# Sums of squares without a POOL adder: one change in three places of a two-layer decoder kernel

## The chip, the cores and the metric

The kernel runs on one core of one Trainium2 chip, in one launch. The metric is the device time of an execution in microseconds (us). The engines are named as in the profile: PE (matrix products), PEld (its weight loads), ACT, DVE and POOL (element-wise work), SP (which starts the DMA transfers). The kernel before takes 683.92 us, the median of three runs (682.63 to 685.81).

## What is computed

Two decoder layers over 512 positions of width 1024, in float32. Cut to what the change touches:

```python
def rmsnorm(x, g):
    return x * rsqrt(mean(x * x, axis=-1) + EPS) * g

# layer 1, latent attention
proj = rmsnorm(x, ln_g) @ w_in                  # 1024 -> 384 + 256 + 32 + 1024
c_q, c_kv, k_rope, gate = split(proj)
q  = rmsnorm(c_q,  q_norm_g)  @ w_q_up          # 16 heads of 96
kv = rmsnorm(c_kv, kv_norm_g) @ w_kv_up         # keys and values, 16 heads of 64
x  = x + (softmax_attention(q, k, v) * silu(gate)) @ w_out
x  = x + sigmoid(x @ ple_w_gate[0]) * (p[0] @ ple_w_proj[0])
# shared keys and values of layer 2, stick-breaking attention
k_sh, v_sh = split(rmsnorm(x, kv_ln_g) @ w_kv_shared)
q, gate = split(rmsnorm(x, sb_ln_g) @ sb_w_in)
x = x + (stick_breaking(q, k_sh, v_sh) * silu(gate)) @ w_out2
x = x + sigmoid(x @ ple_w_gate[1]) * (p[1] @ ple_w_proj[1])
```

Four norms need a sum of squares per position: over x, c_q and c_kv in layer 1, and over the new x in between.

## The kernel before

Activations lie transposed: 128 features on the partitions, 512 positions along a row, so x is 8 tiles (`NK`) and the positions are 4 blocks of 128 (`NT`). Each operand is split into a high part (ACT) and a rest (DVE or POOL), and each product is three matmuls (`mm3`, L132): high by high, high by rest, rest by high. The norm is never applied ahead of a product: its sum of squares is taken beside it, and the factor goes in when the product is read out.

A sum over features is a sum over partitions, which the kernel takes with PE: 128 squares per position as the weights, a column of ones as the moving operand (`self.mm(..., rhs=self.ones[:, 0:1])`). A float32 product of that kind is two passes in the trace.

The order on each engine comes from a scheduler that simulates the program, except where `self.lin` ties every PE instruction to the one ahead of it: at the start (L860 to L892), between the layers (L932 on) and in the second attention layer. The three places of the change lie there.

**Place 1, the start.** `mla_in` (L309) runs over k, the 8 tiles of x. Each k loads a tile of x (L330) and a tile of weights (L335), splits both (L163/L164, L343/L344; from k = 2 on POOL makes the rest of the weights) and issues 15 matmuls into 5 accumulators. ACT also squares each tile of x (L322, L325) and POOL adds the squares up (L326), in turn with its splits. Then the 5 accumulators (3 of c_q, 2 of c_kv) are split and squared; POOL adds the squares again, to one tile for c_q and one for c_kv (L368). After `k_rope` (16 matmuls) `stats` (L372) makes 3 x 4 one-column products from the three sum tiles, and only then `mla_group` (L464) begins: 4 tiles of q, 9 matmuls of 384 columns each, then `k_rotate` (first transposes L423), then keys and values. A generator hands these out in steps of 3 matmuls (`next(first)`).

**Place 2, between the layers.** `out_ple` writes the new x; ACT squares each tile (L926, L929), POOL adds 6 of the 8 squares, three tiles stay (`sqs`). PE makes the first key tile of the shared keys (8 steps, tile g), then 12 one-column products (L947), then the second key tile (8 steps, tile s), then `row_of` (L198) transposes the finished factor into a row. The factor is one small power on POOL (L950); the keys are read out only once the row is there (`self.late`).

**Place 3, the end of the second attention layer.** `sb_layer` (L701) runs 26 turns. Each turn hands out filler steps (`fill`) from a generator of other products, in six parts (`marks`), between scores, transposes (`pt_evac`) and the two products with the values (`av`, L573). In the last turn (i = N + 1) no scores and no transposes are left: two `av` of the last pair of heads and seven filler steps. An `av` needs the rest of its weights from DVE (L571, tile `ptl`).

Of the kernel before, what the change touches and what calls it, by code (L numbers as in the profile page):

```python
# [6 lines left out]
F32 = mybir.dt.float32  # L7
# [9 lines left out]
P = 128  # L17
# [61 lines left out]
class Trunk:  # L79
# [229 lines left out]
    def mla_in(self):  # L309
        nc, A = self.nc, self.A  # L310
        gc = self.const([P, NCOL], F32, "gc")
        self.gc = gc
        MC = (QL + KL) // P
        tags = "ggssttt"
        acc = [self.ps([P, S], x) for x in tags[:MC]]
        xacts = []
        sqx = self.t([P, S], F32, "f")
        xss = []

        def square(k):  # L320
            if k == 0:
                nc.scalar.activation(sqx, xss[k], AF.Square)  # L322
            else:
                sq = self.t([P, S], F32, "f")
                nc.scalar.activation(sq, xss[k], AF.Square)  # L325
                nc.gpsimd.tensor_tensor(out=sqx, in0=sqx, in1=sq, op=ALU.add)  # L326

        for k in range(NK):
            xg = self.t([P, S + 8], F32, "e")[:, 0:S + 1]
            nc.sync.dma_start(out=xg, in_=A["xT"][k])  # L330
            xs, gx = xg[:, 0:S], xg[:, S:S + 1]
            cuts = (0, P, QL + KL) if k == 0 else (0, QL + KL)
            ws = self.t([P, QL + KL], F32, "ws")
            for a, b in zip(cuts, cuts[1:]):
                nc.sync.dma_start(out=ws[:, a:b], in_=A["w_c"][k][:, a:b])  # L335
            if k == 2:
                nc.sync.dma_start(out=gc, in_=A["gain_cols"])
            if k == 0:
                xh, xl = self.split_act(xs, "A", scale=gx)
            wh = self.t([P, QL + KL], F32R, "wh")  # L340
            wl = self.t([P, QL + KL], F32R, "wl")
            for a, b in zip(cuts, cuts[1:]):
                nc.scalar.copy(out=wh[:, a:b], in_=ws[:, a:b])  # L343
                (nc.vector if k < 2 else nc.gpsimd).tensor_tensor(out=wl[:, a:b], in0=ws[:, a:b], in1=f32(wh[:, a:b]),  # L344
                                                                  op=ALU.subtract)
            if k > 0:
                xh, xl = self.split_act(xs, "A", scale=gx)
            xacts.append((xh, xl))
            for m in range(MC):
                self.mm3(acc[m], wh[:, m * P:(m + 1) * P], wl[:, m * P:(m + 1) * P], xh, xl, k == 0, k == NK - 1)  # L350
            xss.append(xs)
            if k > 0:
                square(k - 1)
        square(NK - 1)
        self.xacts = xacts
        self.load_small()
        sqs = []
        lats = []
        for m in range(MC):
            lats.append(self.split_act(acc[m], "B", scale=gc[:, C_QN + m:C_QN + m + 1]))  # L360
            if m in (0, QL // P):
                sq = self.t([P, S], F32, "f")
                nc.scalar.activation(sq, acc[m], AF.Square)
                sqs.append(sq)
            else:
                s2 = self.t([P, S], F32, "f")
                nc.scalar.activation(s2, acc[m], AF.Square)
                nc.gpsimd.tensor_tensor(out=sqs[-1], in0=sqs[-1], in1=s2, op=ALU.add)  # L368
        self.cq, self.ckv = lats[:QL // P], lats[QL // P:]
        self.sums = [sqx] + sqs  # L370

    def stats(self):  # L372
        nc = self.nc
        sps = self.ps([P, 3, NT], "t")
        for i, sq in enumerate(self.sums):
            for t in range(NT):
                self.mm(sps[:, i, t:t + 1], lhsT=sq[:, t * P:(t + 1) * P], rhs=self.ones[:, 0:1], start=True,
                        stop=True)
        st = self.const([P, 3, NT], F32, "stats")
        v = nc.vector  # L380
        v.tensor_copy(out=st, in_=sps)
        w = self.const([P, 8, NT], F32, "statw")
        vx, vq, vkv, exx, euq, t0, skv2, krc = [w[:, i] for i in range(8)]
        v.tensor_scalar(out=vx, in0=st[:, 0], scalar1=1.0 / D, scalar2=EPS, op0=ALU.mult, op1=ALU.add)
        v.tensor_scalar(out=exx, in0=vx, scalar1=EPS, scalar2=None, op0=ALU.mult)
        v.scalar_tensor_tensor(out=vq, in0=st[:, 1], scalar=1.0 / QL, in1=exx, op0=ALU.mult, op1=ALU.add)
        v.scalar_tensor_tensor(out=vkv, in0=st[:, 2], scalar=1.0 / KL, in1=exx, op0=ALU.mult, op1=ALU.add)
        v.tensor_scalar(out=euq, in0=vq, scalar1=EPS, scalar2=None, op0=ALU.mult)
        self.euq = euq
        sx = self.const([P, 2, NT], F32, "sxkv")  # L390
        nc.gpsimd.tensor_tensor(out=sx[:, 0], in0=vx, in1=self.mhalf.to_broadcast((P, NT)), op=ALU.pow)
        nc.gpsimd.tensor_tensor(out=sx[:, 1], in0=vkv, in1=self.mhalf.to_broadcast((P, NT)), op=ALU.pow)
        self.sx, self.skv = sx[:, 0], sx[:, 1]
        v.scalar_tensor_tensor(out=skv2, in0=self.skv, scalar=1.0 / QK, in1=self.skv, op0=ALU.mult, op1=ALU.mult)
        self.skv2 = skv2
        self.krw = (t0, krc)
        hs = self.const([QK, 1], F32, "hs")
        nc.vector.memset(hs, QK ** -0.5)
        nc.vector.scalar_tensor_tensor(out=hs[0:HD], in0=self.hg[0:HD, 0:1], scalar=QK ** -0.5,
                                       in1=self.hg[0:HD, 1:2], op0=ALU.mult, op1=ALU.mult)  # L400
        self.hs = hs
# [299 lines left out]
    def sb_layer(self, windows, pair):  # L701


        NU = 3
        GS = NU * GH // 2
        N = NU * NH // 2
        bs, ready = {}, None
        for i in range(N + 2):
            w = min(i // GS, len(windows) - 1)
            n, gen = windows[w]  # L710
            turns = GS if w < len(windows) - 1 else GS + 2
            step = i - w * GS
            quota = n * (step + 1) // turns - n * step // turns
            marks = [quota * x // 6 for x in range(7)]
            if i == N:
                self.cyc = "gs"

            def fill(a, z):
                for _ in range(marks[z] - marks[a]):
                    next(gen, None)  # L720
            if i < N:
                m, u = divmod(i, NU)
                qs, ks, V = self.groups[i // GS]
                bs[i] = self.sb_front(u, self.sb_scores(u, qs[m], ks[m]))
            fill(0, 1)
            if ready is not None:
                self.av(2 * ready, self.groups[ready // 2][2])
            fill(1, 3)
            b = i - 1
            if 0 <= b < N:  # L730
                e = bs.pop(b)
                self.pt_evac(2 * (b // NU), b % NU, e[0])
            fill(3, 4)
            if ready is not None:
                self.av(2 * ready + 1, self.groups[ready // 2][2])
                pair(ready)
                ready = None
            fill(4, 5)
            if 0 <= b < N:
                self.pt_evac(2 * (b // NU) + 1, b % NU, e[1])  # L740
                if b % NU == NU - 1:
                    ready = b // NU
                if i == N:
                    self.split_later()
            fill(5, 6)
            if step == turns - 1:
                for _ in gen:
                    pass
# [103 lines left out]
    def run(self):  # L852
# [23 lines left out]

        grp = lambda g: self.mla_group(g, self.groups[g])
        self.k_rope()
        self.stats()
        self.rope_tables()  # L880
        self.cyc = SPREAD
        first = grp(0)
        for _ in range(3 * NT):
            next(first)
        self.k_rotate()
        for _ in first:
# [56 lines left out]
            next(first)  # L943
        sps = self.ps([P, NT], "t")
        for t in range(NT):
            for i, sq in enumerate(sqs):
                self.mm(sps[:, t:t + 1], lhsT=sq[:, t * P:(t + 1) * P], rhs=self.ones[:, 0:1], start=i == 0,  # L947
                        stop=i == len(sqs) - 1)
        v.tensor_scalar(out=r2, in0=sps, scalar1=1.0 / D, scalar2=EPS, op0=ALU.mult, op1=ALU.add)
        nc.gpsimd.tensor_tensor(out=r2, in0=r2, in1=self.mhalf.to_broadcast((P, NT)), op=ALU.pow)  # L950
        for _ in range(NK):
            next(first)
        self.R2 = self.row_of(r2)
        for f in self.late:
# [40 lines left out]
def pack(inp):  # L995
# [10 lines left out]

    o = {}
    o["xT"] = c(np.concatenate([f["x"][0].T.reshape(NK, P, S), f["mla_ln_g"][0].reshape(NK, P, 1)], axis=2))
    o["pT"] = c(f["p"][:, 0].reshape(2, S, 2, P).transpose(0, 3, 2, 1))
    o["positions"] = c(f["positions"][0].reshape(NT, P).T)  # L1010
    o["gain_cols"] = c(np.concatenate([cols(f["mla_ln_g"][0]), cols(f["mla_q_norm_g"][0]), cols(f["mla_kv_norm_g"][0]),
# [37 lines left out]
```

## Time and profile before

| | |
|---|---|
| median of three runs | 683.92 us |
| the profiled execution, its own time | 683.51 us |
| its span, first to last instruction | 681.7 us |
| PE busy | 666.2 us, 98% of the span |
| DVE, ACT, POOL busy | 476.7, 400.7, 356.8 us |
| mean granted clock of PE | 0.992 |

The span is what the trace shows; 1.8 us of the execution's time lie around it. PE's busy time is close to the span, so a gain must come out of the few gaps of PE, out of instructions that it runs, or out of the stretches in which it ran at the lower of its two clock levels. A granted clock of 1.00 is 2.4 GHz, 0.50 is 1.2 GHz.

### The profile page before, as it was taken

How to read it: one execution, taken by the hardware profiler on the slowest of the kernel's cores; microseconds unless marked ns; L12 is line 12 of the kernel's file. 1: busy time of each engine (PE TensorE's matmuls, PEld its weight loads, DVE VectorE, ACT ScalarE, POOL GpSimd, SP SyncE). 2: the span in 40 equal slices, each digit the busy share in tenths (PEclk: the TensorE clock that was granted, in tenths of full speed). 3: DMA queues.
4: the chain of work that ended last, by engine and by line, in shares of the span. 5: the costliest groups of instructions: out<-in, count | busy, mean ns of one | idle time of the engine just before them, and what ended most of it. 6: DMA issues, size and time to landing. Idle time of an engine off the chain costs nothing.

```text
span 681.7 us, 10052 instructions
## 1 busy us (share of the span) xinstructions
PE 666.2 (98%) x3598; PEld 560.9 (82%) x3598; DVE 476.7 (70%) x868; ACT 400.7 (59%) x812; POOL 356.8 (52%) x293
## 2 busy tenths in 40 slices
PE   8989999999998999999999999999999999999997
PEld 6778898989877888888789788779879877788886
DVE  6866489987986774846853886876886889654332
ACT  7266496987988664444533666566665777432221
POOL 5737678776795550035443663775856677100130
PEclk9989999999999999999989999999999999999999
DMA  7331302100133110734332222111221222442321
GB/s 242 116 120 56 109 32 66 62 17 17 35 110 105 62 62 32 210 118 136 119 128 62 94 87 67 59 68 34 91 67 59 64 93 84 162 125 93 107 80 62
DMA packets 21762, 59.82 MB, mean 88 GB/s; under 512 B 2896, under 2 KB 3664, under 8 KB 21712
## 3 DMA queue, kind: packets, MB, share of 16 engines
q1 hardware_dynamic: 21712, 59.18, 26.9%
q8 instruction: 28, 0.46, 0.3%
q14 instruction: 22, 0.18, 0.1%
HBM read 54.97 MB, written 4.19 MB: 87 GB/s over the span
## 4 chain that ended last, share of the span: by engine, by line
PE 89%; ACT 4%; DVE 4%; issue 1%; POOL 1%; DMA 0%; ACTq 0%; POOLq 0%
PE g L127 41%; PE t L127 25%; PE s L127 16%; PE t L130 6%; DVE A L161 1%; ACT L447 1%; ACT wh L143 1%; DVE e L609 1%; DVE ptl L571 0%; DMA e<-in_xT 0%; POOL f L326 0%; DVE f L804 0%; ACT L611 0%; ACT f L447 0%; ACT e L611 0%
## 5 line engine op out<-in xcount | busy, mean ns | idle before, releaser
L127 PE MATMUL g<-A,wh 128*128 128x512 f32 x560 | 182.6, 405 | 2.1 <-ACT f L802 1.4
L143 ACT CAST wh<-ws 128x1024 fp32r<-128x1024 f32 (+2 forms) x92 | 90.2, 982 | 106.3 <-issue 41.0
L144 DVE TENSOR_TENSOR wl<-ws,wh 128x1024 fp32r<-128x1024 f32 (+2 forms) x72 | 96.8, 1346 | 47.0 <-ACT wh L143 45.9
L127 PEld LDWEIGHTS g<-A,wh 128*128 128x128 f32 x560 | 99.6, 189 | 25.4 <-issue 3.2
L127 PE MATMUL g<-A,wl 128*128 128x512 f32 x280 | 110.9, 396 | 0.7 <-POOL wl L344 0.7
L182 POOL TENSOR_TENSOR ws<-ws,gc 128x1024 f32<-128x1024 f32 x24 | 52.2, 2177 | 62.7 <-DMA ws<-in_w_sq 25.2
L698 POOL TENSOR_TENSOR e<-e,e 128x384 f32<-128x384 f32 (+1 forms) x48 | 61.9, 1309 | 20.0 <-DVE e L697 17.1
L570 ACT CAST pth<-t 128x384 fp32r<-128x384 f32 (+1 forms) x96 | 49.6, 518 | 32.0 <-PE t L130 31.3
L571 DVE TENSOR_TENSOR ptl<-t,pth 128x384 fp32r<-128x384 f32 (+1 forms) x96 | 56.5, 593 | 14.8 <-ACT pth L570 14.3
L127 PEld LDWEIGHTS g<-A,wl 128*128 128x128 f32 x280 | 52.9, 189 | 13.2 <-POOL wl L344 1.6
L127 PE MATMUL t<-A,wh 128*128 128x512 f32 (+1 forms) x192 | 59.1, 393 | 0.0
L130 PE MATMUL t<-ident,e 128*128 128x128 f32 x320 | 55.4, 272 | 0.0
L697 DVE TENSOR_TENSOR_SCAN e<-e,maskb 128x384 f32<-128x384 f32 (+1 forms) x32 | 45.8, 1471 | 8.2 <-ACT e L686 8.2
L130 PEld LDWEIGHTS t<-ident,e 128*128 128x128 f32 x320 | 40.4, 140 | 7.3 <-POOL e L614 0.2
L144 POOL TENSOR_TENSOR wl<-ws,wh 128x1024 fp32r<-128x1024 f32 (+2 forms) x20 | 40.0, 2002 | 12.2 <-ACT wh L143 10.7
L127 PE MATMUL s<-qk,qk 96*128 96x256 f32 (+1 forms) x192 | 44.4, 338 | 1.4 <-ACT qk L548 0.7
L614 POOL TENSOR_SCALAR e<-e,sm 128x384 f32<-128x384 f32 (+3 forms) x48 | 27.6, 579 | 33.3 <-DVE sm L612 28.7
L611 ACT ACTIVATE e<-e,sm 128x128 f32<-128x128 f32 (+1 forms) x64 | 36.3, 568 | 12.6 <-DVE sm L609 10.8
L127 PE MATMUL g<-wh,B 128*128 128x384 f32 (+1 forms) x136 | 43.4, 376 | 0.3 <-DVE v L538 0.3
L127 PE MATMUL g<-wh,A 128*128 128x256 f32 x208 | 42.4, 289 | 0.0
L127 PEld LDWEIGHTS t<-A,wh 128*128 128x128 f32 (+1 forms) x192 | 35.1, 184 | 8.3
L127 PE MATMUL t<-ptl,v 128*128 128x256 f32 (+2 forms) x128 | 39.5, 329 | 1.8 <-DVE ptl L571 1.8
(291 smaller groups left out, 1607.2 us busy)
## 6 DMA issues: line engine op xcount, KB each, us to landing
ws<-in_w_pg SPq DMA_DIRECT2D x16, 512.0 KB, 3.6
ws<-in_w_g SPq DMA_DIRECT2D x8, 512.0 KB, 3.2
ws<-in_w_o SPq DMA_DIRECT2D x16, 256.0 KB, 2.6
ws<-in_w_k SPq DMA_DIRECT2D x8, 512.0 KB, 3.6
ws<-in_w_sq SPq DMA_DIRECT2D x8, 512.0 KB, 3.5
ws<-in_w_v SPq DMA_DIRECT2D x8, 512.0 KB, 3.6
ws<-in_w_sg SPq DMA_DIRECT2D x8, 512.0 KB, 3.5
ws<-in_w_o SPq DMA_DIRECT2D x8, 512.0 KB, 3.6
```

Of the source, the lines that this page charges most:

```text
L127: return self.pe(self.nc.tensor.matmul(*a, **kw))
L130: return self.pe(self.nc.tensor.transpose(*a))
L143: nc.scalar.copy(out=wh, in_=src)
L144: lo_engine.tensor_tensor(out=wl, in0=src, in1=f32(wh), op=ALU.subtract)
L161: (lo_engine or nc.vector).tensor_tensor(out=lo, in0=src, in1=f32(hi), op=ALU.subtract)
L182: nc.gpsimd.tensor_tensor(out=ws, in0=ws, in1=gain.unsqueeze(2).to_broadcast((P, nk, P)), op=ALU.mult)
L570: nc.scalar.copy(out=views[0], in_=ps)
L571: nc.vector.tensor_tensor(out=views[1], in0=ps, in1=f32(views[0]), op=ALU.subtract)
L611: nc.scalar.activation(e[:, 0:n], e[:, 0:n], AF.Exp, bias=st[:, 0:1], scale=-1.0, accum_out=st[:, 2:3])
L614: nc.gpsimd.tensor_scalar(out=e[:, 0:n], in0=e[:, 0:n], scalar1=st[:, 3:4], scalar2=1.0, op0=ALU.mult, op1=ALU.mult)
L697: v.tensor_tensor_scan(out=x, data0=x, data1=mask[:, ::-1], initial=0.0, op0=ALU.mult, op1=ALU.max)
L698: nc.gpsimd.tensor_tensor(out=b[:, 0:n], in0=b[:, 0:n], in1=om[:, 1:n + 1], op=ALU.mult)
```

## The change

Place 1: the squares of x no longer go through PE and POOL. A second copy of x with the positions on the partitions (`x_rows`, 4 blocks of 128 x 1024, 2.1 MB in all) is loaded after the loads of k = 3, and ACT squares each block in place and adds along the row in the same instruction (`accum_out`). POOL's adds L326 and L368 go; the five squares of c_q and c_kv stay five tiles, and `stats` now makes 4 x (3 + 2) one-column products that accumulate in PSUM. `stats` is moved behind the first tile of q, and after each block of positions it takes a step of the following q tile. The small work on the sum of x (its variance, its power) is free to move ahead of `stats`.

Place 2: before each block's three one-column products a step of the second key tile is taken (4 steps), and after them 9 steps instead of 8, so that `row_of` comes 5 steps later than before, inside the first query tile.

Place 3: in the last turn the first `av` comes two filler steps later, the second three.

```diff
-        sqx = self.t([P, S], F32, "f")
-        xss = []
-        def square(k):
-            if k == 0:
-                nc.scalar.activation(sqx, xss[k], AF.Square)
-            else:
-                sq = self.t([P, S], F32, "f")
-                nc.scalar.activation(sq, xss[k], AF.Square)
-                nc.gpsimd.tensor_tensor(out=sqx, in0=sqx, in1=sq, op=ALU.add)
+        st = self.st = self.const([P, 3, NT], F32, "stats")
+        xr = None
+        def square(t):
+            x = xr[t // 2][:, t % 2]
+            nc.scalar.activation(x, x, AF.Square, accum_out=st[:, 0, t:t + 1])
...
+            if k == 3:
+                xr = [self.t([P, 2, D], F32, "v") for _ in range(2)]
+                for t in range(NT):
+                    nc.sync.dma_start(out=xr[t // 2][:, t % 2], in_=A["x_rows"][t])
+            if k >= NK - NT:
+                square(k - NK + NT)
...
-                nc.gpsimd.tensor_tensor(out=sqs[-1], in0=sqs[-1], in1=s2, op=ALU.add)
+            sq = self.t([P, S], F32, "f")
+            nc.scalar.activation(sq, acc[m], AF.Square)
+            self.sums.append(sq)
...
+    def sum_squares(self, ps, t, sqs):
+        for i, sq in enumerate(sqs):
+            self.mm(ps, lhsT=sq[:, t * P:(t + 1) * P], rhs=self.ones[:, 0:1], start=i == 0, stop=i == len(sqs) - 1)
+    def stats(self, steps):
+        sps = self.ps([P, 2, NT], "t")
+        for t in range(NT):
+            self.sum_squares(sps[:, 0, t:t + 1], t, self.sums[:QL // P])
+            self.sum_squares(sps[:, 1, t:t + 1], t, self.sums[QL // P:])
+            next(steps)
...
+            lag = 2 if i == N + 1 else 0
-            fill(0, 1)
+            fill(0, 1 + lag)
...
-            fill(3, 4)
+            fill(3, 4 + lag)
...
-        self.stats()
         first = grp(0)
-        for _ in range(3 * NT):
+        for _ in range(3):
+            next(first)
+        self.stats(first)
+        for _ in range(3 * NT - 3 - NT):
             next(first)
...
         for t in range(NT):
-            for i, sq in enumerate(sqs):
-                self.mm(...)
+            next(first)
+            self.sum_squares(sps[:, t:t + 1], t, sqs)
...
-        for _ in range(NK):
+        for _ in range(NK - NT + 5):
             next(first)
         self.R2 = self.row_of(r2)
```

How the orders differ: outside the three places PE's order is the same instruction for instruction. PE at place 1 before, from the end of `k_rope` (`wh_396`) to the first q tile (g), with the three sum tiles as f:

```order
L127 MATMUL t_399<-A_331,wh_396 64x512 x2
L127 MATMUL t_418<-ones,f_120 128x1 x4
L127 MATMUL t_418<-ones,f_365 128x1 x4
L127 MATMUL t_418<-ones,f_385 128x1 x4
L127 MATMUL g_506<-wh_499,B_361 128x384
```

The same place now, from the last matmuls of the first q tile (g) into the second (s):

```order
L127 MATMUL g_463<-wh_456,B_358 128x384
L127 MATMUL t_478<-ones,f_369 128x1
L127 MATMUL t_478<-ones,f_371 128x1
L127 MATMUL t_478<-ones,f_373 128x1
L127 MATMUL t_478<-ones,f_375 128x1
L127 MATMUL t_478<-ones,f_377 128x1
L127 MATMUL s_484<-wh_456,B_349 128x384
L127 MATMUL s_484<-wl_457,B_349 128x384
L127 MATMUL s_484<-wh_456,B_350 128x384
L127 MATMUL t_478<-ones,f_369 128x1
```

One block of twelve products ahead of all q tiles has become four blocks of five, with three matmuls between them, behind the first q tile.

ACT in `mla_in` before, at k = 2 to 5 (A is a split tile of x, wh a split weight tile, f a square):

```order
L163 ACTIVATE A_186<-e_177 128x512
L325 ACTIVATE f_233<-e_177 128x512
L343 CAST wh_182<-ws_179 128x640
L163 ACTIVATE A_215<-e_207 128x512
L325 ACTIVATE f_262<-e_207 128x512
L163 ACTIVATE A_244<-e_236 128x512
L325 ACTIVATE f_291<-e_236 128x512
L343 CAST wh_211<-ws_209 128x640
```

ACT at the same k now (v is a block of rows of x, stats the sums):

```order
L163 ACTIVATE A_185<-e_176 128x512
L340 CAST wh_181<-ws_178 128x640
L163 ACTIVATE A_211<-e_203 128x512
L340 CAST wh_207<-ws_205 128x640
L323 ACTIVATE v_229,stats<-v_229 128x1024
L323 ACTIVATE v_229,stats<-v_229 128x1024
L323 ACTIVATE v_230,stats<-v_230 128x1024
L323 ACTIVATE v_230,stats<-v_230 128x1024
L163 ACTIVATE A_243<-e_235 128x512
L340 CAST wh_239<-ws_237 128x640
```

The four row squares stand in one piece ahead of everything that k = 4 needs. On SP their four loads stand at the same point, ahead of the loads of k = 4; on DVE two small operations on the sums and on POOL one power (L387 of the changed kernel) stand ahead of the rests of k = 4.

PE at place 3 before, the third-last step of the last gate (g), the first `av` (t) and the second-last step:

```order
L127 MATMUL g_6249<-A_3602,wh_6245 128x512 x2
L127 MATMUL g_6249<-A_3602,wl_6246 128x512
L127 MATMUL t_6303<-pth_106,v_5590 128x512
L127 MATMUL t_6303<-ptl_108,v_5590 128x512
L127 MATMUL t_6303<-pth_106,v_5590 128x384
...
L127 MATMUL t_6303<-ptl_108,v_5590 128x256
L127 MATMUL g_6249<-A_3644,wh_6245 128x512 x2
```

The same now:

```order
L127 MATMUL g_6241<-A_3636,wh_6237 128x512 x2
L127 MATMUL g_6241<-A_3636,wl_6238 128x512
L127 MATMUL g_6241<-A_3677,wh_6237 128x512 x2
L127 MATMUL g_6241<-A_3677,wl_6238 128x512
L127 MATMUL t_6306<-pth_106,v_5582 128x512
L127 MATMUL t_6306<-ptl_108,v_5582 128x512
```

Both last steps of the gate now stand ahead of the first `av`. At place 2 POOL's order changes by one row: a scaling of the next weights (L182, 128 x 1024) now stands ahead of the power (L950 before).

## Rows read from the trace of the kernel before

**Rows 1.** The page, busy time of an engine.
```profile
PE 666.2 (98%) x3598; PEld 560.9 (82%) x3598; DVE 476.7 (70%) x868; ACT 400.7 (59%) x812; POOL 356.8 (52%) x293
```
**Rows 2.** Waits, the longest: who waited for whom, us in total, times, longest.
```profile
PE t L127 <- POOL f L368: 1.9, 2, 1.2
```
**Rows 3.** Timeline of PE at place 1: start us, us, what, count, idle time before.
```profile
39.89 0.95 PE L127 MATMUL t<-ones,f 128*128 128x1 f32 x8
45.07 0.67 PE L127 MATMUL g<-wh,B 128*128 128x384 f32 x1
52.65 0.33 PE L127 MATMUL g<-wh,B 128*128 128x384 f32 x1
54.03 0.34 PE L127 MATMUL g<-wh,B 128*128 128x384 f32 x1
54.30 0.46 PE L130 MATMUL t<-ident,f 64*128 64x64 f32 x4
```
**Rows 4.** A stretch at place 1: us, busy time of PE, PEld, DVE, ACT, POOL, granted clock.
```profile
46.00:48.00 2.00, 2.00 (x8) 2.00 (x7) 0.70 (x5) 0.00 (x0) 1.96 (x2) 0.50 0.00 0
```
**Rows 5.** Timeline of ACT in `mla_in`.
```profile
4.29 0.61 ACT L322 ACTIVATE f<-e 128x512 f32<-128x512 f32 x1
4.80 0.82 ACT L343 CAST wh<-ws 128x128 fp32r<-128x128 f32 x2
13.57 0.71 ACT L343 CAST wh<-ws 128x640 fp32r<-128x640 f32 x1
14.18 0.72 ACT L163 ACTIVATE A<-e 128x512 fp32r<-128x512 f32 x1
```
**Rows 6.** Timeline of PE in `mla_in`: its first matmul, and k = 4.
```profile
5.14 1.22 PE L127 MATMUL g<-A,wh 128*128 128x512 f32 x2 [0.58 <-ACT wh L343]
21.60 0.61 PE L127 MATMUL g<-A,wh 128*128 128x512 f32 x2
22.94 0.50 PE L127 MATMUL g<-A,wl 128*128 128x512 f32 x1 [0.72 <-POOL wl L344]
```
**Rows 7.** Timeline of POOL at k = 4.
```profile
18.38 3.00 POOL L326 TENSOR_TENSOR f<-f,f 128x512 f32<-128x512 f32 x2
21.33 1.55 POOL L344 TENSOR_TENSOR wl<-ws,wh 128x640 fp32r<-128x640 f32 x1
```
**Rows 8.** DMA from 0 to 80 us, GB/s in 40 slices of 2 us.
```profile
GB/s 11 265 221 274 344 403 342 72 128 37 127 12 152 70 223 90 272 238 252 66 207 39 227 0 0 0 4 8 4 205 90 0 0 129 178 217 0 0 230 65
```
**Rows 9.** ACT's instructions by shape: count, busy us, mean ns.
```profile
L143 ACT CAST wh<-ws 128x1024 fp32r<-128x1024 f32 x72 | 75.8, 1052 | 93.3 <-issue 40.1 <-PE t L127 21.5 <-PE s L127 16.2
L611 ACT ACTIVATION_READ_ACCUMULATOR e<-e,sm 128x1 f32 x64 | 12.5, 195 | 0.0
```
**Rows 10.** Timeline of PE at place 2.
```profile
341.73 2.73 PE L127 MATMUL t<-ones,f 128*128 128x1 f32 x24
344.33 0.86 PE L127 MATMUL s<-A,wh 128*128 128x512 f32 x2
348.75 0.63 PE L127 MATMUL s<-A,wh 128*128 128x512 f32 x2
351.51 0.60 PE L130 MATMUL t<-ident,r 128*128 128x128 f32 x4
```
**Rows 11.** A stretch at place 2.
```profile
346.00:348.00 2.00, 2.00 (x7) 1.54 (x6) 0.54 (x2) 0.00 (x0) 0.72 (x1) 0.50 0.49 147
```
**Rows 12.** Timeline of POOL at place 2.
```profile
349.14 1.02 POOL L950 TENSOR_TENSOR r<-r,mhalf 128x4 f32<-128x4 f32 x1
350.19 1.94 POOL L182 TENSOR_TENSOR ws<-ws,gc 128x1024 f32<-128x1024 f32 x1
```
**Rows 13.** Timeline of PE at place 3: a step of the gate, and the first `av`.
```profile
578.04 0.62 PE L127 MATMUL g<-A,wh 128*128 128x512 f32 x2
578.74 0.39 PE L127 MATMUL t<-pth,v 128*128 128x512 f32 x1
580.96 0.50 PE L127 MATMUL t<-ptl,v 128*128 128x512 f32 x1 [1.82 <-DVE ptl L571]
```

More of the change, by code (lines that the diff above doesn't have):

```diff
@@ L350, in mla_in @@
                 self.mm3(acc[m], wh[:, m * P:(m + 1) * P], wl[:, m * P:(m + 1) * P], xh, xl, k == 0, k == NK - 1)
[L351 to L354, printed above, removed]
+            if k == 3:
[4 more added lines that the diff above has]
+                square(k - NK + NT)
@@ L355, in mla_in @@
         self.xacts = xacts
         self.load_small()
-        sqs = []
-        lats = []
+        lats = [self.split_act(acc[m], "B", scale=gc[:, C_QN + m:C_QN + m + 1]) for m in range(MC)]
+        self.cq, self.ckv = lats[:QL // P], lats[QL // P:]
+        self.sums = []
         for m in range(MC):
[L360 to L367, printed above, removed]
-                nc.gpsimd.tensor_tensor(out=sqs[-1], in0=sqs[-1], in1=s2, op=ALU.add)
@@ L369, in mla_in @@
-        self.cq, self.ckv = lats[:QL // P], lats[QL // P:]
-        self.sums = [sqx] + sqs
-    def stats(self):
-        nc = self.nc
[L374 to L379, printed above, removed]
+            sq = self.t([P, S], F32, "f")
+            nc.scalar.activation(sq, acc[m], AF.Square)
@@ new lines, in mla_in @@
+            self.sums.append(sq)
[3 more added lines that the diff above has]
+    def stats(self, steps):
+        nc = self.nc
+        sps = self.ps([P, 2, NT], "t")
[3 more added lines that the diff above has]
+            next(steps)
+        st = self.st
@@ L380, in stats @@
         v = nc.vector
-        v.tensor_copy(out=st, in_=sps)
+        v.tensor_copy(out=st[:, 1:3], in_=sps)
         w = self.const([P, 8, NT], F32, "statw")
@@ L724, in sb_layer @@
                 bs[i] = self.sb_front(u, self.sb_scores(u, qs[m], ks[m]))
-            fill(0, 1)
+            lag = 2 if i == N + 1 else 0
+            fill(0, 1 + lag)
             if ready is not None:
                 self.av(2 * ready, self.groups[ready // 2][2])
-            fill(1, 3)
+            fill(1 + lag, 3)
             b = i - 1
@@ L737, in sb_layer @@
                 ready = None
-            fill(4, 5)
+            fill(4 + lag, 5)
             if 0 <= b < N:
@@ L744, in sb_layer @@
                     self.split_later()
-            fill(5, 6)
+            fill(max(5, 4 + lag), 6)
             if step == turns - 1:
@@ L945, in run @@
         for t in range(NT):
-            for i, sq in enumerate(sqs):
-                self.mm(sps[:, t:t + 1], lhsT=sq[:, t * P:(t + 1) * P], rhs=self.ones[:, 0:1], start=i == 0,
-                        stop=i == len(sqs) - 1)
+            next(first)
+            self.sum_squares(sps[:, t:t + 1], t, sqs)
         v.tensor_scalar(out=r2, in0=sps, scalar1=1.0 / D, scalar2=EPS, op0=ALU.mult, op1=ALU.add)
         nc.gpsimd.tensor_tensor(out=r2, in0=r2, in1=self.mhalf.to_broadcast((P, NT)), op=ALU.pow)
-        for _ in range(NK):
+        for _ in range(NK - NT + 5):
             next(first)
@@ L1008, in pack @@
     o["xT"] = c(np.concatenate([f["x"][0].T.reshape(NK, P, S), f["mla_ln_g"][0].reshape(NK, P, 1)], axis=2))
+    o["x_rows"] = c(f["x"][0].reshape(NT, P, D))
     o["pT"] = c(f["p"][:, 0].reshape(2, S, 2, P).transpose(0, 3, 2, 1))
```

## The prediction

> **What bounds the kernel now.** I read the page's busy times first, then the list of who waited for whom, then PE's timeline with the granted clock of short stretches, then the engines that PE waits for. PE is busy for 666.2 us of the span [rows 1], so a change pays only where PE idles, where it runs fewer or other instructions, or where it runs at 1.2 GHz. The three places hold some of each. At place 1 PE waits for POOL's adder of squares, 1.9 us in two waits [rows 2]. Between the end of `k_rope` at 39.89 and the transposes of `k_rotate` at 54.30 PE needs 14.41 us for 24 one-column passes and 36 matmuls of the q tiles [rows 3], and in that stretch the clock is at its lower level, 0.50 from 46 to 48 us [rows 4]. At place 2 PE never idles, but behind 24 one-column passes it falls to 0.50 too [rows 10, 11]. At place 3 it waits 1.82 us inside an `av` for DVE [rows 13].
>
> **Start of place 1, `mla_in`.** ACT's first square (L322) stands ahead of the cast of the first weights; without it the cast can start at 4.29 and not 4.80 [rows 5], and PE's first matmul, at 5.14 [rows 6], moves forward by up to 0.5 us. Its second needs the rest of x from DVE, which does not move. Bounds 0 and 0.5; I take 0.4, since ACT is what PE waits for there. At k = 4 PE waits 0.72 us for the rest of the weights [rows 6]; POOL was late with it because two adds of 3.0 us stood ahead [rows 7]. They go: 0.7 us, provided nothing else is late at k = 4.
>
> What could be late is new: the rows of x. Ahead of them 4 tiles of x (262.7 KB each) and 4 of weights (327.7 KB) are loaded, 2.36 MB. The transfers moved 2.23 MB in the first 10 us (five slices of 2 us), then 403 and 342 GB/s [rows 8]. So 2.36 MB are in at about 10.3 us, and the 2.10 MB of rows at a mean of 372 GB/s take 5.6 us more, to 15.9. A square of 1024 columns is not in the trace; the nearest is ACT's cast of that shape, 1.05 us, and the read of a row sum, 0.20 us [rows 9]. The last square is over at 17.2, ACT's split and cast for k = 4 (0.7 us each, [rows 5]) at 18.6, POOL's rest (1.55 us, [rows 7]) at 20.2; the power that now stands ahead of it on POOL (1.02 us, the shape of L950 in [rows 12]) fits in while ACT splits. PE starts k = 4 at 21.60 now [rows 6], 0.4 us earlier in the changed kernel: 1.0 us to spare. Behind the squares on ACT, behind two small operations on DVE, and behind the row loads on SP stand all operands of k = 4 to 7, and PE waits for those in order, so what is late beyond that 1.0 us costs its full length. I take nothing.
>
> **Place 1, the sums.** A one-column pass takes 0.108 us at 2.4 GHz (24 of them from 341.73 to 344.33, [rows 10]), a matmul of 384 columns 0.1725 us (eight from 52.65 to 54.03, [rows 3]). Now there are 20 products, 40 passes: 40 x 0.108 = 4.33 us, and 36 x 0.1725 = 6.21 us, together 10.54 us without a wait and at full clock. Against 14.41 us that saves 3.87 us. It is made of two waits that go (1.9 us), of 16 passes more (-1.7 us), and of the clock: 27 matmuls of the q tiles took 7.58 us from 45.07 to 52.65 instead of 4.66, so 2.9 us, with some more lost on the passes. So most of this term hangs on the clock. What is late next: the first block of sums needs the five squares, of which the last stands on ACT behind a cast that waits for the end of `k_rope`; by a cast of 1.05 us [rows 9] and a square of 0.6 us [rows 5] it is there 1.7 us after that end, while PE first has nine matmuls (1.6 us) and then six passes of the other tiles. No wait. One new wait: the five squares and the tile of `k_rope` fill all six buffers f, so ACT's square of the first q tile waits until the last block of sums has read the first one, and the copies of the q tiles queue behind it. PE's next three tiles go to other PSUM buffers; the first that needs this one is the third tile of keys, about 4 us after ACT has caught up. Hidden.
>
> **Place 2.** Between 344.33 and 351.51 stand 8 steps, 7.18 us; at full clock a step is 0.69 us (four from 348.75 to 351.51, [rows 10]), so 5.52 us. If the clock holds, 1.66 us are saved; the passes stay 24. The cost is on the other side: the row of norms needs the power, and POOL now has a scaling of 1.94 us ahead of it [rows 12]. By the order, sums end at 341.73 + 4 x (0.69 + 0.65) = 347.1, and `row_of` comes nine steps later, at 353.3. POOL's scaling started at 350.19 before [rows 12]; if it cannot start earlier, it ends at 352.1 and the power at 353.15. That is even; I charge 0.2 us, bounds 0 and 1. The keys are read out about 2 us later, far ahead of the scores that need them, which come after the query and value tiles.
>
> **Place 3.** Two steps of 0.70 us (578.04 to 578.74, [rows 13]) move into the 1.82 us wait: 1.4 us. DVE's work ahead of the awaited operation does not move. The second `av` comes three steps later; its output is the last of eight parts of the next product, which starts with the other seven. Bounds 0 and 1.8.
>
> **Sum.** 0.4 + 0.7 + 3.9 + 1.7 - 0.2 + 1.4 = 7.9 us. The profiled execution took 683.51 us, so 675.6; it lies 0.4 us under the median of the runs, so **676.0 us**.
>
> **A rule against the rows.** At place 2 the rows show PE busy without a gap and yet at 1.2 GHz behind the passes [rows 10, 11]. The Trainium skill (TensorE: Matmul & The Clock Gate, section Why this matters for your kernels) names idle gaps between bursts of matmuls as what takes the clock away. By that rule one-column passes are harmless and place 1 is safe once its two waits are gone: the sum would be the same 676.0, but with the chance of the first rival below added to it. By the rows 677.7 to 678.9 stays open. The trace contradicts the rule at place 2, which by it should not have fallen at all, so I let the rows decide and keep that rival.
>
> **Rivals.**
> First: the clock falls at place 1 all the same. For it: passes alone brought it down at place 2, and the changed kernel has 40 of them here in four runs of ten, with only three matmuls between. Against it: none of the runs is as long as the 24, and both idle waits are gone. Price: as much as place 2 lost (1.66 us) to as much as place 1 lost (2.9 us). That gives 677.7 to 678.9 us.
> Second: place 2 does not do what it is moved for: the clock falls although the passes come in four runs of six. Against it: full steps as long as the passes stand between. Price 1.66 us: 677.7 alone, with the first rival 679.4 to 680.6.
> Third, the slower side: the row loads starve k = 4. For it: they stand in one queue ahead of the loads of k = 4 to 7, and ACT, DVE and POOL all stop behind them. Against it: 403 and 342 GB/s in the very slices in which they would run. From 1.0 us of lateness on each us costs one; to eat the gain takes 8.9 us, that is 2.1 MB in 14.5 us or 145 GB/s. The trace has such slices (72 and 128 GB/s right behind the burst, [rows 8]), though with less asked for. At 100 GB/s the rows would take 21 us, 15.4 more than reckoned, so 14.4 us of waiting: 690 us.
>
> **How the numbers follow.** Forecast, clock held at both: 0.50. First rival: 0.30. Second alone 0.07, both falls 0.05. Third 0.08, of which about half with a stall of 1 to 7 us that leaves the kernel faster or even, and 0.04 slower. The range runs from 1.6 us under the forecast (half the 3.2 us between the three runs of before; the terms' own bounds below are smaller, 0.1 at the start, 0.2 at place 2, 0.4 at place 3) to the falls above: 674.4 to 680.4. Measurements of this kernel can tell about 0.5%, 3.4 us, from no change, so faster means under 680.5: the forecast, the first rival, the second alone and part of the rest, 0.88; same 0.08; slower 0.04.
>
> **What would show it.** In the changed profile: no POOL wait on the one-column products; the granted clock in the stretch after `k_rope` at 1.00 throughout (right) or at 0.50 for some us (first rival); the distance from the last `k_rope` matmul to the first transposes near 10.5 us; no wait of PE at k = 4 for ACT or POOL, with the last row square over near 17 us; clock 1.00 behind the passes at place 2 and at most a few tenths of waiting at `row_of`; the wait inside the first `av` of the last turn down to about 0.4 us. It would be wrong in its ground if PE waited in `mla_in` for more than before, or if a wait appeared where PE's order did not change.

## The result: 680.03 us, half of the forecast gain

The changed kernel takes 680.03 us (median of nine runs, 678.05 to 682.47); the kernel before took 683.92 beside it (682.14 to 685.81). The ratio is 0.9946, 95% interval 0.9930 to 0.9963: 3.9 us faster where 7.9 were forecast. The profiled execution took 680.42 us.

The page of the changed kernel, its busy times:

```profile
PE 666.4 (98%) x3614; PEld 561.8 (83%) x3614; DVE 467.5 (69%) x868; ACT 401.3 (59%) x812; POOL 340.6 (50%) x283
```

POOL lost 16 us and ten instructions, PE has 16 passes more, and PE is as busy as before [rows 1]. The list of who PE waited for has no line for POOL's adder any more [rows 2]; of its lines one stands at place 1, and one just ahead of place 3, at 575.32, where PE's order is as before:

```profile
PE g L127 <- POOL wl L341: 0.9, 1, 0.9
PE t L130 <- POOL e L694: 0.4, 1, 0.4
```

**Start.** The timeline of PE in `mla_in`, its first product, the first pairs, and k = 4:

```profile
4.62 1.39 PE L127 MATMUL g<-A,wh 128*128 128x512 f32 x2
7.19 0.62 PE L127 MATMUL s<-A,wh 128*128 128x512 f32 x2
...
19.69 0.70 PE L127 MATMUL g<-A,wh 128*128 128x512 f32 x2
21.29 0.50 PE L127 MATMUL g<-A,wl 128*128 128x512 f32 x1 [0.89 <-POOL wl L341]
```

PE starts 0.5 us earlier [rows 6], and a pair of products takes 0.62 us from 7.19 on; before, pairs took 1.05 us until 10.2. A pair of this shape takes 1.05 us elsewhere at a granted clock of 0.50 (at 24.62 in no_sums, below), so before PE ran at 1.2 GHz up to there, although the clock column reads 1.00 in these first microseconds. With both, PE begins k = 4 at 19.69, 1.9 us earlier than before. But the wait for POOL's rest at k = 4 is still there, and larger. ACT and POOL show why:

```profile
13.36 1.06 ACT L323 ACTIVATE v<-v 128x1024 f32<-128x1024 f32 x1 [0.49 <-DMA v<-in_x_rows]
...
18.20 0.18 ACT L323 ACTIVATION_READ_ACCUMULATOR v<-v 128x1 f32 x1
18.29 0.71 ACT L163 ACTIVATE A<-e 128x512 fp32r<-128x512 f32 x1
```

```profile
18.67 1.03 POOL L387 TENSOR_TENSOR sxkv<-statw,mhalf 128x4 f32<-128x4 f32 x1 [4.14 <-DVE statw L380]
19.69 1.54 POOL L341 TENSOR_TENSOR wl<-ws,wh 128x640 fp32r<-128x640 f32 x1
```

The four row squares end at 18.4, not at 17.2, and all that k = 4 needs stands behind them: ACT's split at 18.29, and POOL's rest of the weights (L341), which starts at 19.69, behind the power (L387).

**Place 1.** The timeline of PE from the end of `k_rope` to the first transposes (the runs of ten passes, and some rows between):

```profile
38.24 0.34 PE L127 MATMUL g<-wh,B 128*128 128x384 f32 x1
...
39.83 1.17 PE L127 MATMUL t<-ones,f 128*128 128x1 f32 x10
...
41.47 1.17 PE L127 MATMUL t<-ones,f 128*128 128x1 f32 x10
...
43.11 1.28 PE L127 MATMUL t<-ones,f 128*128 128x1 f32 x10
44.25 0.67 PE L127 MATMUL s<-wh,B 128*128 128x384 f32 x1
...
45.36 2.13 PE L127 MATMUL t<-ones,f 128*128 128x1 f32 x10
...
52.27 0.46 PE L130 MATMUL t<-ident,f 64*128 64x64 f32 x4
```

No row has a wait, and still it takes 14.03 us (38.24 to 52.27) against 14.41 [rows 3]. The first two runs of passes take 1.17 us, the last 2.13. The windows (us; busy time of PE, PEld, DVE, ACT and POOL; granted clock; DMA share and GB/s) give the reason:

```profile
42.00:44.00 2.00, 2.00 (x18) 2.00 (x17) 1.47 (x10) 0.43 (x2) 0.00 (x0) 1.00 0.72 254
44.00:46.00 2.00, 2.00 (x10) 2.00 (x10) 0.03 (x1) 0.12 (x1) 0.00 (x0) 0.51 0.02 8
46.00:48.00 2.00, 2.00 (x9) 2.00 (x10) 1.00 (x5) 1.63 (x6) 0.00 (x0) 0.50 0.05 12
48.00:50.00 2.00, 2.00 (x8) 2.00 (x7) 0.67 (x3) 0.00 (x0) 1.01 (x1) 0.50 0.02 4
50.00:52.00 2.00, 2.00 (x11) 2.00 (x10) 0.55 (x1) 0.93 (x3) 0.00 (x0) 0.79 0.00 0
```

PE is busy in every microsecond, and from 44 to about 51 it runs at 1.2 GHz. That is as long as before, where [rows 4] is one window of such a fall: the granted clock was 0.59 from 44 to 46 us, 0.50 up to 50 and 0.70 from 50 to 52.

**Places 2 and 3.** At place 2 the same window as [rows 11], and `row_of`:

```profile
346.00:348.00 2.00, 2.00 (x11) 1.71 (x12) 0.16 (x1) 0.00 (x0) 1.45 (x1) 1.00 0.67 166
```

```profile
341.50 0.72 PE L127 MATMUL t<-ones,f 128*128 128x1 f32 x6
...
352.39 0.60 PE L130 MATMUL t<-ident,r 128*128 128x128 f32 x4
```

Full clock, no wait at `row_of`. At place 3 the wait inside the first `av` [rows 13] is gone:

```profile
578.59 0.40 PE L127 MATMUL t<-pth,v 128*128 128x512 f32 x1
578.82 0.39 PE L127 MATMUL t<-ptl,v 128*128 128x512 f32 x1
```

### The profile page after: what moved, and what is told of

Its sections match the earlier page's. It is cut to its first block, busy times and chain, and to the rows that moved or that the text cites. A ratio compares the mean times of both kernels' runs of the same rounds, so it can differ in the third digit from the quotient of the medians.

```text
span 678.4 us, 10074 instructions
## 1 busy us (share of the span) xinstructions
PE 666.4 (98%) x3614; PEld 561.8 (83%) x3614; DVE 467.5 (69%) x868; ACT 401.3 (59%) x812; POOL 340.6 (50%) x283
## 4 chain that ended last, share of the span: by engine, by line
PE 84%; DVE 8%; ACT 4%; issue 2%; DMA 1%; POOL 1%; ACTq 0%; DVEq 0%; SPq 0%; POOLq 0%
PE g L127 38%; PE t L127 25%; PE s L127 16%; PE t L130 6%; DVE e L693 2%; DVE wl L144 1%; DVE ptl L567 1%; DMA ws<-in_pT 1%; DVE e L605 1%; DVE A L161 1%; ACT L443 1%; POOL e L694 0%; DMA e<-in_xT 0%; ACT L607 0%; ACT f L443 0%
## 5 line engine op out<-in xcount | busy, mean ns | idle before, releaser
L144 DVE TENSOR_TENSOR wl<-ws,wh 128x1024 fp32r<-128x1024 f32 (+2 forms) x72 | 100.7, 1400 | 42.4 <-ACT wh L143 40.0
L182 POOL TENSOR_TENSOR ws<-ws,gc 128x1024 f32<-128x1024 f32 x24 | 50.4, 2100 | 66.4 <-DMA ws<-in_w_sq 26.3
L127 PE MATMUL g<-wh,B 128*128 128x384 f32 (+1 forms) x136 | 42.5, 368 | 0.3 <-DVE v L534 0.3
L127 PE MATMUL t<-pth,v 128*128 128x256 f32 (+2 forms) x128 | 41.1, 331 | 0.0
```

The costliest lines, as they stand in the source:

```text
L127: return self.pe(self.nc.tensor.matmul(*a, **kw))
L144: lo_engine.tensor_tensor(out=wl, in0=src, in1=f32(wh), op=ALU.subtract)
L182: nc.gpsimd.tensor_tensor(out=ws, in0=ws, in1=gain.unsqueeze(2).to_broadcast((P, nk, P)), op=ALU.mult)
```

## The experiments

Ratios are to the kernel before, measured beside each run. Edits are to the changed kernel where nothing else is said. Two theories stood against each other. C: the missing gain went into PE's lower clock at place 1, and the one-column passes bring it down. L: the passes themselves cost more than reckoned.

### Is it the clock, and which property of the passes?

**spread_sums**: twice as many matmuls between the blocks of passes.

```diff
             self.sum_squares(sps[:, 1, t:t + 1], t, self.sums[QL // P:])
             next(steps)
+            next(steps)
```

> The changed kernel with two steps of q tiles (six matmuls) between the blocks of sums at place 1 instead of one; the same 20 products, the same 36 matmuls. Theory C (PE's lower clock is what ate the gain; it fell because ten passes had only three matmuls between): passes then take about as much time as the matmuls between them (10 x 0.108 against 6 x 0.1725 us), as at place 2 of the changed kernel, where the clock held; granted clock 1.00 throughout, the stretch from the last k_rope matmul to the first transposes 10.6 us instead of 14.03, time 3.4 us less: 676.6 us. Rival L (the 40 passes themselves cost more than reckoned, wherever they stand): stretch 14, time 680. Rival W (a fall comes with any passes within such a stretch): clock 0.50 somewhere from 42 to 52 us, time 678 to 680.

Measured: 676.87 us, ratio 0.9902 (0.9865 to 0.9938). The median is C's number, the profile is not: the clock falls once, later, as the last run of passes ends.

```profile
44.00:46.00 2.00, 2.00 (x17) 2.00 (x16) 0.07 (x1) 0.00 (x0) 0.00 (x0) 1.00 0.04 16
46.00:48.00 2.00, 2.00 (x15) 2.00 (x15) 0.72 (x4) 1.27 (x5) 0.00 (x0) 0.85 0.04 12
48.00:50.00 2.00, 2.00 (x8) 2.00 (x7) 1.33 (x6) 1.31 (x6) 1.01 (x1) 0.50 0.00 0
50.00:52.00 2.00, 2.00 (x10) 1.36 (x10) 0.73 (x2) 1.29 (x4) 0.52 (x2) 0.80 0.01 4
```

The six runs spread from 673.81 to 682.74, with mean granted clocks of the whole execution from 1.000 down to 0.987. In this profile the fall is about half as long as in the changed kernel, and two runs have a mean of 1.000: spacing makes it rarer or shorter, not impossible. Rival W's fall is in this profile, its time (678 to 680) is not.

**wide_sums**: the order of the changed kernel, with 64 columns in place of one.

```diff
-            self.mm(ps, lhsT=sq[...], rhs=self.ones[:, 0:1], ...)
+            self.mm(ps, lhsT=sq[...], rhs=self.ones[:, 0:ps.shape[-1]], ...)
...
-        sps = self.ps([P, 2, NT], "t")
+        sps = self.ps([P, 2, NT, 64], "t")
...
-        v.tensor_copy(out=st[:, 1:3], in_=sps)
+        v.tensor_copy(out=st[:, 1:3], in_=sps[:, :, :, 0])
```

> The changed kernel with a moving operand of 64 columns of ones in place of one at place 1; everything else in the same order. It asks whether it is the single column that takes the clock down. Theory C in that form: a pass takes as long as before (it is bounded by its weights) or a little longer, the clock stays at 1.00, the stretch takes 10.5 to 12 us instead of 14.03, time 676.5 to 678. Rival: the fall has to do with the passes' float32 weights and not with the columns; the clock falls as before, stretch 14 or more, time 680 or more.

Measured: 675.82 us, ratio 0.9882 (0.9859 to 0.9904), six runs within 674.50 to 677.03, a little faster than expected. PE's timeline and windows:

```profile
39.71 1.22 PE L127 MATMUL t<-ones,f 128*128 128x64 f32 x10
...
44.64 1.22 PE L127 MATMUL t<-ones,f 128*128 128x64 f32 x10
...
48.98 0.46 PE L130 MATMUL t<-ident,f 64*128 64x64 f32 x4
```

```profile
44.00:46.00 2.00, 2.00 (x17) 2.00 (x17) 0.41 (x1) 0.93 (x4) 0.00 (x0) 1.00 0.22 88
46.00:48.00 2.00, 2.00 (x13) 2.00 (x12) 1.17 (x7) 1.24 (x5) 1.01 (x1) 1.00 0.06 12
```

Ten passes of 64 columns take 1.22 us, as good as the 1.17 of ten with one column, the clock stays at 1.00, and the stretch takes 38.12 to 48.98, 10.86 us. Nothing but the number of columns differs, so this shows C, and in its narrow form: it is the passes with a single column, called empty passes from here on. L falls: 40 passes stand here too. Two later profiles repeat it: late_rows_wide, with 64 columns, has no fall at place 1, and place1_alone, with one column, falls from 42.5 to 52.7 us.

**no_sums**: no products at all; this kernel leaves the sums out.

```diff
-            self.sum_squares(sps[:, 0, t:t + 1], t, self.sums[:QL // P])
-            self.sum_squares(sps[:, 1, t:t + 1], t, self.sums[QL // P:])
...
-        v.tensor_copy(out=st[:, 1:3], in_=sps)
+        v.memset(st[:, 1:3], 100.0)
```

> The changed kernel without the 20 one-column products at place 1; the sums are set to a constant (this part of the computation is left out). Theory C: stretch 36 x 0.1725 = 6.2 us instead of 14.03, clock 1.00, time 7.8 us less: 672.2 us. Rival L': the clock falls there for another reason (what stands ahead of the passes): 0.50 for some us all the same, stretch 9 or more, time 675 or more.

Measured: 672.55 us, ratio 0.9838 (0.9814 to 0.9863). The stretch takes 6.36 us (40.92 to 47.28) at full clock, as C has it: nothing ahead of the passes takes the clock there. All the passes together lengthen the stretch by 4.5 us where the clock holds (10.86 - 6.36); the medians differ by 3.3 only (675.82 - 672.55), since no_sums loses time at k = 4. That is the edit's doing: with constant sums POOL's second power, which comes at 48.04 in the changed kernel, is free to run early, and it stands ahead of the rest of k = 4 too. PE's wait grows to 2.05 us, and the clock falls behind it.

```profile
19.52 1.07 POOL L385 TENSOR_TENSOR sxkv<-statw,mhalf 128x4 f32<-128x4 f32 x1
...
22.33 0.50 PE L127 MATMUL g<-A,wl 128*128 128x512 f32 x1 [2.05 <-POOL wl L341]
...
24.62 1.05 PE L127 MATMUL s<-A,wh 128*128 128x512 f32 x2
```

```profile
22.00:24.00 2.00, 1.67 (x6) 1.38 (x7) 2.00 (x2) 0.94 (x2) 2.00 (x3) 0.85 0.28 63
24.00:26.00 2.00, 2.00 (x6) 1.51 (x6) 2.00 (x3) 0.00 (x0) 1.76 (x1) 0.50 0.54 171
```

**before_wide**: the kernel before, with wide columns alone.

```diff
-                self.mm(sps[:, i, t:t + 1], lhsT=sq[...], rhs=self.ones[:, 0:1], ...)
+                self.mm(sps[:, i, t], lhsT=sq[...], rhs=self.ones[:, 0:40], ...)
...
-                self.mm(sps[:, t:t + 1], lhsT=sq[...], rhs=self.ones[:, 0:1], ...)
+                self.mm(sps[:, t], lhsT=sq[...], rhs=self.ones[:, 0:64], ...)
```

> The kernel before with the one column of ones widened, to 40 columns at place 1 and 64 at place 2, and nothing else: POOL's adds, the two waits of 1.9 us at place 1, the blocks of twelve products in one piece all stay. If it is the single column that takes the clock down and not the idle time or the 24 passes in one run: granted clock 1.00 at both places, 2.9 us less at place 1 and 1.7 at place 2, so 683.0 - 4.6 = 678.4 us. Rival (the waits in PE's stream do it, as the rule on idle gaps has it): place 1 still falls for about 7 us, only place 2 holds, 681.3. Rival: nothing changes, 683.

Measured: 682.27 us, ratio 0.9989 (0.9965 to 1.0013). The first rival, in the profile: place 2 holds, with its 24 passes still in one piece; place 1 falls, in the second of PE's two waits (0.71 already from 42 to 44 us, and slow passes from 43.66 on). The times alone cannot tell it from no change.

```profile
41.45 1.09 PE L127 MATMUL t<-ones,f 128*128 128x40 f32 x8 [0.73 <-POOL f L368]
43.66 1.93 PE L127 MATMUL t<-ones,f 128*128 128x40 f32 x8 [1.12 <-POOL f L368]
```

```profile
42.00:44.00 2.00, 0.88 (x7) 0.76 (x6) 0.79 (x4) 1.64 (x3) 1.60 (x1) 0.71 0.24 49
44.00:46.00 2.00, 2.00 (x10) 2.00 (x10) 1.55 (x11) 0.26 (x1) 0.00 (x0) 0.50 0.53 217
...
346.00:348.00 2.00, 2.00 (x10) 1.66 (x9) 1.45 (x2) 0.00 (x0) 0.29 (x1) 1.00 0.69 248
```

So two things can take the clock: at place 1 of the kernel before most likely idle time, at place 2 most likely empty passes. Neither is shown as cleanly as the fall in the changed kernel. At place 1 no run takes the waits away and leaves all else, and 40 columns were not tried without waits. At place 2 the clock falls behind the 24 one-column passes in two of the three profiles that have them in one piece (before and place1_alone, not place3_alone), and in none of the eight that have them in four runs of six. The 1.7 us that place 2 should give do not stand out of the noise of this kernel's runs (678.47 to 686.88).

### What do fewer passes and later rows give?

**pooled_latents**: POOL adds the squares of c_q and c_kv again, 8 products in place of 20, behind two q tiles.

```diff
-            self.sums.append(sq)
+            if m in (0, QL // P):
+                self.sums.append(sq)
+            else:
+                nc.gpsimd.tensor_tensor(out=self.sums[-1], in0=self.sums[-1], in1=sq, op=ALU.add)
...
-            self.sum_squares(sps[:, 1, t:t + 1], t, self.sums[QL // P:])
+            self.sum_squares(sps[:, 1, t:t + 1], t, self.sums[1:])
...
-        for _ in range(3):
+        for _ in range(6):
             next(first)
         self.stats(first)
```

> The changed kernel with the latent squares added on POOL again (three adds), so 8 one-column products instead of 20, and the sums behind two q tiles instead of one. Theory C: 16 x 0.108 + 36 x 0.1725 = 7.9 us for the stretch and no fall of the clock, less up to 0.8 us of waiting for POOL's third add: 6 us less than 680.0, so 674 to 675. Rival L (only the passes cost): 24 passes of 0.108 us go, 2.6 us, so 677.4. If PE waits for POOL as in the kernel before (1.9 us in two waits) and the clock falls: 679 to 680.

Measured: 674.94 us, ratio 0.9868 (0.9840 to 0.9896): C's number. The stretch takes 9.24 us (38.17 to 47.41), of which 0.93 is a wait for POOL's third add; the clock holds, in spite of that wait.

```profile
42.52 0.38 PE L127 MATMUL t<-ones,f 128*128 128x1 f32 x2 [0.93 <-POOL f L365]
...
47.41 0.46 PE L130 MATMUL t<-ident,f 64*128 64x64 f32 x4
```

**late_rows_wide** and **late_rows_pooled**: the rows of x are loaded behind the last load of `mla_in` and squared behind ACT's last cast there; the second, which is pooled_latents otherwise, also takes a seventh step ahead of the sums.

```diff
+            self.tc.add_manual_dep(sq.ins, cast.ins.name, ...)
...
-            if k == 3:
+            if k == NK - 1:
                 xr = [...]
...
-            if k >= NK - NT:
-                square(k - NK + NT)
+        for t in range(NT):
+            square(t)
```

> The wide_sums kernel with the rows of x loaded behind all loads of mla_in and squared behind ACT's last cast there; place 1 otherwise as in wide_sums. If the row squares make the wait at k = 4: that wait (0.8 us in wide_sums) goes, 675.8 - 0.8 = 675.0, and the runs spread less. Rival: the k = 4 wait stays, or a wait of the same size comes at the first q tile: 675.8 or more.

> The pooled_latents kernel with two more edits: the rows of x are loaded behind all loads of mla_in and squared on ACT behind its last cast of weights there (so nothing of k = 4 to 7 stands behind them), and the sums come one step of q tiles later. If the wait at k = 4 (0.89 us in the changed kernel, 2.1 in no_sums) is the row squares' doing: no wait of PE for POOL at k = 4, no wait for POOL's third add (0.93 us in pooled_latents, at most 0.4 now), clock 1.00 at place 1; 674.9 less 0.9 and 0.5 to 0.9, so 673 to 674 us. Rival: POOL is late at k = 4 anyway, or the squares now hold back ACT's splits of the latents (four of 1.25 us ahead of them): PE waits at the first q tile, 675 to 677.

Measured: 675.51 (ratio 0.9874, 0.9852 to 0.9896) and 672.81 us (0.9833, 0.9810 to 0.9856). In neither does PE wait at k = 4; the timeline of late_rows_pooled there, and ACT's first row square:

```profile
20.16 0.61 PE L127 MATMUL g<-A,wh 128*128 128x512 f32 x2
20.61 0.39 PE L127 MATMUL g<-A,wl 128*128 128x512 f32 x1
```

```profile
24.40 1.06 ACT L323 ACTIVATE v<-v 128x1024 f32<-128x1024 f32 x1
```

So the rows make that wait: their squares on ACT, and the power that follows them on POOL. The loads of the rows, which the third rival feared, do not: in the changed kernel ACT goes from the last square to the split of k = 4 (18.29) without a wait for a transfer. The wait also depends on when PE arrives. In pooled_latents the squares stand as in the changed kernel and POOL's rest of k = 4 ends at about the same time (21.2), but PE, held up by ACT at 9.69, begins k = 4 only at 20.47 and hardly waits. With the wide sums the 0.8 us do not show in the median (0.3 us, inside both intervals). The second kernel gains 2.1 us on pooled_latents, of which 0.93 is the wait for POOL's add.

### The places apart

**place1_alone** sets places 2 and 3 back; **places23_alone** and **place3_alone** put them into the kernel before.

```diff
-            lag = 2 if i == N + 1 else 0
+            lag = 0
...
-            next(first)
             self.sum_squares(sps[:, t:t + 1], t, sqs)
...
-        for _ in range(NK - NT + 5):
+        for _ in range(NK):
```

> The changed kernel with places 2 and 3 set back as before; only place 1 is changed. By the comparison of the two profiles place 1 with its start gave 1.65 + 0.38 = 2.0 us: 684.2 - 2.0 = 682.2, the clock falling once at place 1 and once at place 2. By the sum of the prediction it would be 5.0 us, 679.2.

> The kernel before with places 2 and 3 of the change; place 1 as before. By the comparison of the profiles place 2 gave 1.6 and place 3 2.0 us, and the second attention layer lost 0.9 in between: 684.2 - 2.7 = 681.5 if that loss belongs to the change, 684.2 - 3.6 = 680.6 if it is chance. The clock falls at place 1 and not at place 2.

> The kernel before with the last turn's order alone changed. By the prediction 1.4 us (two steps of 0.70 in a wait of 1.82), 681.6; by the comparison of the two profiles up to 2.0 us, 681.0, since the whole wait went. Rival: the later av delays what follows it, 0 to 0.5 us, 682.5 to 683.

Measured: 682.11 us, ratio 0.9975 (0.9956 to 0.9993); 680.14 us, 0.9940 (0.9920 to 0.9959); 681.91 us, 0.9976 (0.9954 to 0.9998). By the ratios and 683.4 us place 1 gave 1.7 us (0.5 to 3.0), places 2 and 3 gave 4.1 (2.8 to 5.5), place 3 of these 1.6 (0.1 to 3.1). The parts add to 5.8 us, the whole change gave 3.9; the difference lies within these intervals. In the profile of place3_alone, where place 2 is as before, the clock falls behind a wait of PE for ACT, ahead of the passes (from 342.43), and the same 24 one-column passes then run at full clock with no fall behind them:

```profile
335.21 0.73 PE L127 MATMUL g<-A,wh 128*128 128x512 f32 x2 [2.06 <-ACT f L803]
```

```profile
336.00:338.00 2.00, 2.00 (x8) 1.56 (x7) 1.97 (x3) 0.40 (x2) 0.93 (x1) 0.67 0.00 0
338.00:340.00 2.00, 2.00 (x6) 1.61 (x5) 1.90 (x4) 1.69 (x6) 0.00 (x0) 0.50 0.38 82
```

**all_together**: late_rows_pooled with 64 columns at places 1 and 2.

> late_rows_pooled with 64 columns of ones at places 1 and 2. The clock already held at both places there in the profiled run; if it falls there in some other runs, the median drops by a part of 1.7 us and the runs spread less: 671.5 to 672.8 us. Rival: the wider products cost what they save, 672.8 or more.

Measured: 672.01 us (671.26 to 673.32), ratio 0.9835 (0.9807 to 0.9864): 8.0 us under the changed kernel by the medians, 7.6 by the ratios. Against late_rows_pooled it is inside the noise.

## Why the prediction was half right

- **Place 1, the sums, 3.9 us: wrong.** The step that failed is "40 x 0.108 + 36 x 0.1725 = 10.54 us without a wait and at full clock". The sum and "no wait" were right: wide_sums took 10.86 us for the same order. The full clock was not given, and the term came to 0.4 us in the profile. With the clock held (wide_sums) the whole kernel takes 675.8 us, and 676.0 was forecast: this assumption carries the miss. That the two numbers agree so well is luck in part: the 0.7 us of k = 4 did not come there either, and the clock's earlier rise at the start, which nobody forecast, stood in for them in its profile.
- **The first rival** is what happened. I held against it that no run of passes was as long as the 24 of place 2, and that the waits were gone. Four runs of ten passes with three matmuls between brought it down all the same, in the changed kernel and in place1_alone. Its price was set too low as well: 1.66 to 2.9 us, measured 14.03 - 10.54 = 3.5 us in the profile, and 4.2 us between the medians of wide_sums and the changed kernel. The range's upper end, 680.4, was to reach both falls, which the rivals put at up to 680.6.
- **The rule on idle gaps** (the Trainium skill, TensorE: Matmul & The Clock Gate, Why this matters for your kernels): before_wide goes its way in part. At place 1 the clock falls in the second of two waits although no pass is empty, but the waits, 0.73 and 1.12 us, are shorter than the gaps which that section warns of. The changed kernel, beside wide_sums, shows a fall in a stretch without any idle time, which the section does not have. Removing the waits most likely removed one of two causes and brought in more of the other.
- **k = 4, 0.7 us: wrong.** The forecast was that POOL's wait goes and that 1.0 us was to spare. The wait stayed, 0.89 us. Two estimates were short: the squares end at 18.4 and not at 17.2 (the first starts at 13.36, and each holds ACT for 1.28 us from start to start), and PE itself reached k = 4 at 19.69 and not at 21.2, since the clock rose earlier at the start. The first used up the 1.0 us, the second made the wait. That the rows cause it is shown by the two kernels with late rows. The third rival had the place right and the cause wrong: the squares were slow, not the loads, at a small part of its price.
- **Start, 0.4 us: about right**, 0.5 measured. `k_rope` ended 1.65 us earlier than before in all, 1.1 forecast; the rest came from PE's faster pairs from 7.19 on, which were not forecast and are not bound to the change. In all_together, whose first products are those of the changed kernel, the pairs are slow up to 10.3; in before_wide, which starts as the kernel before, they take 0.73 us at 7.31 and 0.63 from 8.38 on.

```profile
7.82 1.06 PE L127 MATMUL s<-A,wh 128*128 128x512 f32 x2
```

- **Place 2, 1.7 - 0.2 us: right in the profiled runs**: full clock behind the passes, no wait at `row_of`, 1.6 us between the profiles. That the passes alone brought the clock down there, as the prediction read [rows 10, 11], is not fully shown: in place3_alone the fall stood ahead of them, behind a wait, and the passes ran at full clock.
- **Place 3, 1.4 us: right in size**, 1.6 us alone (0.1 to 3.1). "DVE's work ahead of the awaited operation does not move" held in order, not in time: the wait that [rows 13] show at 1.82 us is 0.6 us in the profiles of before_wide and place1_alone, where nothing there was changed. One of the prediction's own signs of being wrong also appeared, in a small way: a wait where PE's order did not change, 0.4 us for POOL at 575.32. place1_alone and place3_alone have it too, and its cause stays open.
- **The rest**: between the two profiles PE wins 1.65 us up to the end of `k_rope`, 0.4 at place 1, 1.6 at place 2 and 2.0 at place 3. It loses 1.0 in the first attention layer, where the clock falls at about 208 us in the changed kernel and not in the kernel before, and 0.9 in the second. By PE's last product 3.6 us are left. Neither loss was forecast. places23_alone, with the same order in the second layer, does not lose there, so that part is chance as far as the profiles tell.

What stays open: how long a stretch of one-column passes a given spacing can carry. spread_sums fell in one profile and had runs at a mean clock of 1.000.

## What to carry to other kernels

A stretch without idle time is not yet a stretch at full clock: where a kernel sums over partitions with a column of ones, widen the column as long as the pass does not get longer (64 columns cost 1.22 us for ten passes, one column 1.17), or make fewer passes. Before counting a gain that hangs on the clock, ask of the new stretch what brought the old one down, and look for both causes, waits and empty passes. Work that is moved off the critical engine into another engine's fixed order belongs behind what the critical engine still waits for there, not at the point where its data are first there.

## What the runs showed of the hardware beyond that

- A float32 pass of 64 columns is as good as free beside one of a single column: from the first of ten passes to the matmul behind them it is 1.03 us with either (39.71 to 40.74 in wide_sums, 39.83 to 40.86 in the changed kernel).
- Falls of the clock come and go where the instructions are the same: six of the profiles (the changed kernel, pooled_latents, both with late rows, place1_alone, before_wide) show one between 202 and 214 us, behind PE's wait of 2.0 to 2.1 us for DVE's gate; the others, that of before among them, have the same wait and no fall. That of the changed kernel:

```profile
206.00:208.00 2.00, 0.74 (x3) 0.66 (x4) 1.23 (x3) 1.95 (x6) 1.53 (x3) 0.97 0.07 25
208.00:210.00 2.00, 2.00 (x6) 1.52 (x6) 1.94 (x4) 1.25 (x3) 1.49 (x2) 0.50 0.04 9
```

- A row sum on ACT is two instructions: the square of 1024 columns, 1.06 us, and the read of the sum, 0.18 to 0.19 us.
